# Second FFN's gate and up projections as seven half-size block products per pair of tiles, with the block sums on VectorE

## The chip, the cores and the metric

The kernel runs as one program on one core of a Trainium2 chip. The metric is the device time of one execution in microseconds; lower is better. A core has TensorE (matmuls, called PE in the profile, with its weight loads as PEld), VectorE (DVE), ScalarE (ACT), GpSimd (POOL) and SyncE (SP), which here issues the loads and stores. Each engine works through its own instructions in the order in which they stand, and semaphores make one wait for another.

## What is computed

Two layers of a diffusion backbone over 512 latent tokens, with 256 context tokens beside them in the first layer. Model width is 1024, the hidden width of the FFN 2816. Cut to the part that is changed, the second layer ends with

```python
h_lat = h_lat + g1 * o_lat
a = modulate(rms_norm(h_lat, norm_ffn_g[i]), sh2, sc2)
h_lat = h_lat + g2 * ((silu(a @ ffn_w_gate[i]) * (a @ ffn_w_up[i])) @ ffn_w_down[i])
```

where `a` is 512 x 1024, the gate and up weights are 1024 x 2816 each, and the down weight is 2816 x 1024. Everything is float32.

## The kernel before, in words

A float32 product is made of three matmuls of type fp32r: each operand is split into a high part (a cast) and a low part (the operand minus the cast), and high x high, high x low and low x high are summed in PSUM. Activations lie transposed: channels on the 128 partitions, tokens along the free dimension.

`Weights` streams the weights. A tile of 128 x 1024 float32 is loaded by SP (L134) into one of three raw buffers, cast on ScalarE (L136), and its low part is made on VectorE, or on GpSimd while `W.eng` says so (L137). Four split buffers hold the results, and splits run about two tiles ahead of their use.

The last stage ("stage C", from L1066) begins when the attention of layer two has ended. First comes the output projection `wo_mm` (tiles `pw`, L1102 to L1104), output tiles 0 to 3 with 512 columns, then 4 to 7 in two token halves HA and HB of 256 columns. `updater` adds each into `h` (L555). `Norm.sq` squares on ScalarE (L171) and sums on VectorE (L172, tile `accC`), `Norm.ms` and `Norm.rb` make the root and spread it with small matmuls, and `Norm.apply` makes for each of 8 channel tiles `u` (VectorE, L204), the high part `ahC` (ScalarE, L206) and the low part `alC` (VectorE, L207). During this part `WC.eng` is GpSimd.

Then the FFN. The hidden width is 22 tiles of 128 (j = 0 to 21). For each tile there is a gate unit and an up unit: 8 channel tiles x 3 matmuls of 128 x 128 weights against 512 token columns (`unit_mm`, L118 to L120, PSUM tile `pu`). `first_units` makes the first three units in halves, so that they can start before HB is normed. `elementwise` makes silu (L332), the product (L334), and the split of the result into `hc` (L337, L338). `Down.run` multiplies finished hidden tiles in groups (2, then 4 at a time) by the down weights (PSUM tile `pd`, 512 columns), one group behind the projections. `last_one` does the last four tiles (`pk`, `pd`).

The orders of TensorE and SP are those in which the code is written (`manual_schedule`); those of VectorE, ScalarE and GpSimd are set by a scheduler when the program is built.

Of the kernel before, what the change touches and what calls it, by code (L numbers as in the profile page):

```python
# [11 lines left out]
F32 = mybir.dt.float32  # L12
# [39 lines left out]
def tile_trunk(ctx, tc, hT, cols, rows, rope, mod0, modw, cin, cout, gu, dn0, dn1, dnt, kvin, qin,  # L52
# [4 lines left out]
    hid = ctx.enter_context(tc.tile_pool(name="hid", bufs=1))  # L57
# [102 lines left out]
    class Norm:  # L160
        def __init__(self, layer, sub, hof, acc, tmp, ps):
            self.l, self.s, self.hof, self.acc, self.tmp, self.ps = layer, sub, hof, acc, tmp, ps
            self.x, self.r = {}, {}

        def sq(self, j, st):
            n = width(st)
            if j == 0:
                nc.scalar.activation(out=self.acc[:, st], in_=self.hof(j, st), func=AF.Square)
            else:
                t = self.tmp.tile([P, TL], F32, tag="sq", name="sq")  # L170
                nc.scalar.activation(out=t[:, :n], in_=self.hof(j, st), func=AF.Square)  # L171
                (nc.gpsimd if self.l == 0 and self.s == 0 and st is CTX else nc.vector).tensor_tensor(out=self.acc[:, st], in0=self.acc[:, st], in1=t[:, :n], op=ALU.add)  # L172
# [24 lines left out]
        def apply(self, j, st, ah, al):  # L197
# [5 lines left out]
            u = self.tmp.tile([P, TL], F32, tag="u", name="u")  # L203
# [16 lines left out]
    def first_units(W, n, ah, al, pspool, norm, early):  # L220
        ws = [W.get() for _ in range(n)]
        full = [pspool.tile([P, TL], F32, tag="ps", name="pu") for _ in range(n)]
        res = [{LAT.start: p} for p in full]
        for e, st in enumerate(early):
            for i in range(n):
                if st is CTX:
                    res[i][CTX.start] = pspool.tile([P, TL], F32, tag="ps", name="pu")
                unit_mm(res[i][CTX.start] if st is CTX else full[i][:, st], ws[i], ah, al, st)
                if e == 0 and i == 0:
                    norm.ms(HB)  # L230
                if e == 0 and i == 1:
                    norm.rb(HB)
                    for j in range(ND):
                        norm.apply(j, HB, ah, al)
# [13 lines left out]
    class Down:  # L248
# [24 lines left out]
        def k_outer(self, gi, ws, chunks, st, ms):  # L273
# [3 lines left out]
            for ks in (range(K - 1), (K - 1,)):  # L277
# [310 lines left out]
    o = op.tile([P, ND, TL], F32, name="o")  # L588
    wkv = ctx.enter_context(tc.tile_pool(name="wkv", bufs=1, side="right", reuse_waits="tile"))
# [473 lines left out]
    stB.close()  # L1063

    stC = ExitStack()
    actC = pool(stC, "actC", 1)  # L1066
    ahC = actC.tile([P, ND, TL], F32R, name="ahC")
    alC = actC.tile([P, ND, TL], F32R, name="alC")
    tmpC = pool(stC, "tmpC", 2)
    wrawC = pool(stC, "wrawC", 3)  # L1070
    whlC = pool(stC, "whlC", 4)
    oneC = pool(stC, "oneC", 1)
    psC = pool(stC, "psC", 8, space=PSUM)
    WC = Weights(wrawC, whlC)
    WC.add(wo3[3], 768)
    for m in range(3, ND):
        WC.add(wout[m - 3], 1024)
    ffn_units(WC, 1, dn1)
    table(AF.Silu, live[NI - 1][1][:, 2:3])
    accC = oneC.tile([P, T], F32, name="accC")  # L1080
    oc = []
    for c in range(ND):
        if c < 6:
            oc.append(hid.tile([P, 2, T], F32R, tag="hc", name="hc", bufs=6)[:, :, :TL])
        else:
            oc.append(oneC.tile([P, 2, TL], F32R, name=f"oc{c}"))
# [25 lines left out]
    for i in range(4):  # L1112
        upd(i, LAT, pss[i])
        norm.sq(i, HA)
        norm.sq(i, HB)
    WC.eng = nc.gpsimd
    ws = {m: WC.get() for m in range(4, ND)}
    for st in (HA, HB):
        for i in range(4):
            ps = psC.tile([P, TL], F32, tag="ps", name="pw")  # L1120
# [5 lines left out]
            if st is HB and i == 1:  # L1126
                norm.rb(HA)
                for j in range(ND):
                    norm.apply(j, HA, ahC, alC)
    units = first_units(WC, 3, ahC, alC, psC, norm, (HA,))  # L1130
    WC.eng = nc.vector

    def done(m, st):
        nc.sync.dma_start(out=out[m, :, st], in_=h[:, m, st])

    ffn(WC, 1, ahC, alC, psC, tmpC, (LAT,), updater(1, 5), units, lambda j: None,
        lambda down, gi, chunks: down.last_one(gi, chunks, done))
# [91 lines left out]
```

## Time and profile before

| what | value |
|---|---|
| median of 3 runs | 1661.02 us (1660.96 to 1661.17) |
| span of the profiled execution | 1660.0 us |
| own time of the profiled execution | not listed apart from its span; the runs are 1.0 us above the span |
| PE busy | 1599.6 us, 96% of the span, 9634 matmuls |
| DVE, ACT, POOL busy | 57%, 34%, 14% |
| stage C up to the first unit's HB half | 1233 to 1297 us |
| projections of tile 1 to the start of `last_one` | 1305 to 1634 us |

A busy time is the sum of the recorded durations of an engine's instructions. Matmuls overlap, so their durations say less than the distance from the start of one to the start of the next; this distance is used below for TensorE. The profile's slices of the span give busy shares in tenths and the TensorE clock that was granted.

### The profile page before, as it was taken

The page shows a single profiled execution, that of the slowest core. Times are in us where ns is not written, and L with a number is a line of the kernel's source. Part 1 is how long each engine was busy: PE and PEld are TensorE (multiplying, and loading weights), DVE is VectorE, ACT ScalarE, POOL GpSimd, SP SyncE. Part 2 cuts the span into 40 slices and gives each one's busy share as a digit, 9 for nine tenths or more (in the row PEclk, how much of TensorE's full clock was granted, in tenths as well). Part 3 has the DMA queues.
Part 4 walks back from the last instruction along what each step waited for, and adds up shares of the span by engine and source line. Part 5 has one row for each costly group of instructions (what it writes and reads, how often), then busy time and mean ns, then how long its engine had stood idle before and what let it go on. Part 6 is the DMA issues. An engine that isn't in the chain of part 4 may idle for free.

```text
span 1660.0 us, 23829 instructions
## 1 busy us (share of the span) xinstructions
PE 1599.6 (96%) x9634; PEld 1409.1 (85%) x9634; DVE 946.8 (57%) x1624; ACT 570.2 (34%) x1058; POOL 230.4 (14%) x280
## 2 busy tenths in 40 slices
PE   4999999899999999999999988999989999999999
PEld 3888889898888888888899978988878888888887
DVE  3898654858464443533257488778876443334343
ACT  3422122421212112121235557777763322222221
POOL 4000001200000000000014134566513000000000
PEclk9999999999999999999999999999999999999999
DMA  7565331134234242421103111000022222232231
GB/s 290 201 214 178 115 114 52 52 125 155 102 140 140 102 149 93 143 98 64 58 16 99 46 35 42 1 23 27 1 87 85 77 89 98 93 96 95 90 101 64
DMA packets 47022, 159.81 MB, mean 96 GB/s; under 512 B 5120, under 2 KB 6544, under 8 KB 46784
## 3 DMA queue, kind: packets, MB, share of 16 engines
q1 hardware_dynamic: 46816, 158.06, 27.9%
q8 instruction: 76, 1.25, 0.3%
q0 software_dynamic: 96, 0.23, 0.1%
q14 instruction: 34, 0.28, 0.1%
HBM read 156.17 MB, written 2.10 MB: 95 GB/s over the span
## 4 chain that ended last, share of the span: by engine, by line
PE 87%; DVE 6%; ACT 2%; POOL 2%; issue 1%; DMA 0%; ACTq 0%; DVEq 0%; POOLq 0%
PE pu L119 15%; PE pu L118 15%; PE pu L120 15%; PE pd L118 7%; PE pd L119 7%; PE pd L120 7%; PE pp L1008 2%; PE pp L1021 1%; PE s L985 1%; PE s L984 1%; PE s L983 1%; DVE al L207 1%; PE pp L1020 1%; PE pu L217 1%; PE pw L1104 1%
## 5 line engine op out<-in xcount | busy, mean ns | idle before, releaser
L136 ACT CAST wh<-wr 128x1024 fp32r<-128x1024 f32 (+2 forms) x180 | 186.7, 1038 | 587.9 <-PE pu L120 228.6
L118 PE MATMUL pu<-ah,wh 128*128 128x256 f32 (+1 forms) x1040 | 347.8, 334 | 0.0
L119 PE MATMUL pu<-al,wh 128*128 128x256 f32 (+1 forms) x1040 | 347.6, 334 | 0.0
L120 PE MATMUL pu<-ah,wh 128*128 128x256 f32 (+1 forms) x1040 | 347.5, 334 | 0.0
L137 DVE TENSOR_TENSOR wh<-wr,wh 128x1024 fp32r<-128x1024 f32 (+1 forms) x152 | 187.2, 1233 | 217.2 <-ACT wh L136 216.9
L118 PE MATMUL pd<-hc,wh 128*128 128x256 f32 (+1 forms) x676 | 228.4, 338 | 0.0
L119 PE MATMUL pd<-hc,wh 128*128 128x256 f32 (+1 forms) x676 | 227.9, 337 | 0.0
L120 PE MATMUL pd<-hc,wh 128*128 128x256 f32 (+1 forms) x676 | 227.3, 336 | 0.0
L119 PEld LDWEIGHTS pu<-al,wh 128*128 128x128 f32 x1040 | 196.4, 189 | 22.4
L118 PEld LDWEIGHTS pu<-ah,wh 128*128 128x128 f32 x1040 | 196.2, 189 | 22.4
L120 PEld LDWEIGHTS pu<-ah,wh 128*128 128x128 f32 x1040 | 196.4, 189 | 22.2
L508 DVE CUSTOM_DVE_ANT_0 junk<-modr,cb 128x1024 f32<-128x1024 f32 x128 | 156.2, 1221 | 58.3 <-DMA modr<-in_modw 57.3
L137 POOL TENSOR_TENSOR wh<-wr,wh 128x1024 fp32r<-128x1024 f32 (+1 forms) x28 | 63.8, 2289 | 843.5 <-ACT wh L136 843.4
L119 PE MATMUL pu<-alC,wh 128*128 128x512 f32 (+1 forms) x352 | 138.3, 393 | 2.7 <-DVE alC L207 2.7
L118 PEld LDWEIGHTS pd<-hc,wh 128*128 128x128 f32 x676 | 128.3, 190 | 14.4
L119 PEld LDWEIGHTS pd<-hc,wh 128*128 128x128 f32 x676 | 128.4, 190 | 13.9
L120 PEld LDWEIGHTS pd<-hc,wh 128*128 128x128 f32 x676 | 128.2, 190 | 14.1
L555 DVE SCALAR_TENSOR_TENSOR h<-pd,M,h 128x512 f32<-128x512 f32 (+1 forms) x125 | 84.2, 675 | 96.4 <-PE pd L120 96.4
L118 PE MATMUL pu<-ahC,wh 128*128 128x512 f32 (+1 forms) x352 | 138.1, 392 | 0.4 <-ACT ahC L206 0.4
L120 PE MATMUL pu<-ahC,wh 128*128 128x512 f32 (+1 forms) x352 | 137.8, 391 | 0.0
L334 DVE TENSOR_TENSOR sg<-sg,pu 128x256 f32<-128x256 f32 (+1 forms) x66 | 39.5, 598 | 146.1 <-PE pu L120 128.2
L332 ACT ACTIVATE sg<-pu 128x256 f32<-128x256 f32 (+1 forms) x66 | 34.8, 528 | 207.1 <-PE pu L120 207.1
(233 smaller groups left out, 2780.5 us busy)
## 6 DMA issues: line engine op xcount, KB each, us to landing
wr<-in_gu SPq DMA_DIRECT2D x88, 512.0 KB, 3.5
modr<-in_modw SPq DMA_DIRECT2D x80, 512.0 KB, 4.3
wr<-in_dn SPq DMA_DIRECT2D x40, 512.0 KB, 3.5
wr<-in_cin SPq DMA_DIRECT2D x24, 512.0 KB, 4.6
mw<-in_mod SPq DMA_DIRECT2D x16, 512.0 KB, 9.4
wrb<-in_qup SPq DMA_DIRECT2D x12, 384.0 KB, 3.1
wr<-in_cout SPq DMA_DIRECT2D x8, 512.0 KB, 4.0
wr<-in_qin SPq DMA_DIRECT2D x6, 512.0 KB, 3.6
```

The costliest lines, as they stand in the source:

```text
L118: nc.tensor.matmul(ps, wh, xh, start=i == 0, stop=False)
L119: nc.tensor.matmul(ps, wh, xl, start=False, stop=False)
L120: nc.tensor.matmul(ps, wl, xh, start=False, stop=i == n - 1)
L136: nc.scalar.copy(out=w[:, 0, :n], in_=r[:, :n])
L137: (eng or self.eng).tensor_tensor(out=w[:, 1, :n], in0=r[:, :n], in1=w[:, 0, :n].bitcast(F32), op=ALU.subtract)
L207: nc.vector.scalar_tensor_tensor(out=al[:, j, st], in0=u[:, :n], scalar=sh, in1=ah[:, j, st].bitcast(F32), op0=ALU.add, op1=ALU.subtract)
L217: nc.tensor.matmul(ps, wh, al[:, k, st], start=False, stop=False)
L332: nc.scalar.activation(out=sg[:, st], in_=g[st.start][:, :width(st)], func=AF.Silu)
L334: nc.vector.tensor_tensor(out=sg[:, st], in0=sg[:, st], in1=u[st.start][:, :width(st)], op=ALU.mult)
L508: nc.vector.tensor_tensor_reduce(out=junk, in0=r, in1=cb[:, st], scale=1.0, scalar=0.0, op0=ALU.mult, op1=ALU.add, accum_out=M[:, l, st, s ...
L555: nc.vector.scalar_tensor_tensor(out=hof(m, st), in0=ps, scalar=M[:, layer, i, s, m:m + 1], in1=hof(m, st), op0=ALU.mult, op1=ALU.add)
L1008: nc.tensor.transpose(ps[:, e], pr[:, tok(3 * b + e)], ident)
```

## The change

Tiles 0 and 1 are computed as before. Tiles 2 to 21 are computed in ten pairs. For a pair, gate and up are each a product of a 256 x 1024 weight block by a 1024 x 512 activation block. Each is cut in two by two: the weights into A11, A12 (tile p, first and second 512 channels) and A21, A22 (tile q), the activations into B11, B12, B21, B22 (channel half, token half). Seven products of a 128 x 512 block by a 512 x 256 block replace eight, in a form of Strassen's method (Winograd's variant).

- The activation sums t1 to t4 are made once (`combo`), on VectorE with casts on ScalarE. They need the whole `a` in float32, so `Norm.apply` writes a copy `af` with a second activation per tile.
- The weight sums are made per pair on VectorE, in place in the raw tiles (`Stream.pair`, `add`), before the split of the block.
- The result blocks are put together in PSUM by accumulating several products into one bank (A), with copies out to SBUF between them (ScalarE), and sums on VectorE (tile `c`).
- `Stream` replaces `Weights` in stage C: blocks of 512 columns, 7 raw buffers, 9 split buffers, splits up to 8 blocks ahead. The splits under `WC.eng` on GpSimd become 14 of half size in place of 7.
- `last_one` leaves the last two hidden tiles of its group to the end in its first half, not the last one (`late=2`).
- Pools are opened in another order, so that `hid` and `wkv` give their memory back before stage C.

The core of the diff:

```diff
+        def half(self):
+            while len(self.ready) <= self.ahead and self.todo:
+                self._split()
+            return self.ready.pop(0)
...
+            for step in range(7):
+                for p, q in ids:
+                    a11, a12, a21, a22 = (p, 0), (p, 512), (q, 0), (q, 512)
+                    if step == 0:
+                        self.block(*a11, 512)
+                    elif step == 1:
+                        self.block(*a12, 512)
+                    elif step == 2:
+                        self.block(*a21, 512, chain(add(a11, a11, a21), add(a21, a21, a22)))
+                    elif step == 3:
+                        self.block(*a21, 512, add(a21, a11, a22))
+                    elif step == 4:
+                        self.block(*a11, 512)
+                    elif step == 5:
+                        self.block(*a22, 512)
+                    else:
+                        self.block(*a12, 512, chain(add(a12, a12, a21), done(p, 2), done(q, 1)))
...
             nc.scalar.activation(out=ah[:, j, st], in_=u[:, :n], func=AF.Identity, bias=sh)
             nc.vector.scalar_tensor_tensor(out=al[:, j, st], in0=u[:, :n], scalar=sh,
                                            in1=ah[:, j, st].bitcast(F32), op0=ALU.add, op1=ALU.subtract)
+            if full is not None:
+                nc.scalar.activation(out=full[:, j, st], in_=u[:, :n], func=AF.Identity, bias=sh)
...
-    wrawC = pool(stC, "wrawC", 3)
-    whlC = pool(stC, "whlC", 4)
+    wrawC = pool(stC, "wrawC", 7)
+    whlC = pool(stC, "whlC", 9)
...
+    combo(B[0, 0], t1[:, 0], t1[:, 1], lambda: nc.vector.tensor_tensor(
+        out=B[0, 0], in0=B[0, 0], in1=B[0, 1], op=ALU.subtract))
...
+    def product(ps, x, first=False):
+        w = WC.half()
+        xh, xl = X[x]
+        for k in range(4):
+            wh, wl = w[:, 0, k * P:(k + 1) * P], w[:, 1, k * P:(k + 1) * P]
+            nc.tensor.matmul(ps, wh, xh[:, k], start=first and k == 0, stop=False, skip_group_check=not first)
+            nc.tensor.matmul(ps, wh, xl[:, k], start=False, stop=False, skip_group_check=not first)
+            nc.tensor.matmul(ps, wl, xh[:, k], start=False, stop=k == 3, skip_group_check=not first)
...
+        for g in range(2):
+            product(A[g], "b11", True)
+            nc.scalar.copy(out=cs_[g][:, 0], in_=A[g])
+        Bk = bank()
+        for g in range(2):
+            product(Bk[g], "b21", True)
+            nc.vector.tensor_tensor(out=cs_[g][:, 0], in0=cs_[g][:, 0], in1=Bk[g], op=ALU.add)
+        Dk = bank()
+        for g in range(2):
+            product(Dk[g], "t1", True)
+        for g in range(2):
+            product(A[g], "t2")
+            nc.scalar.copy(out=cs_[g][:, 1], in_=A[g])
+        for g in range(2):
+            product(A[g], "t3")
+            nc.scalar.copy(out=cs_[g][:, 2], in_=A[g])
+            nc.vector.tensor_tensor(out=cs_[g][:, 2], in0=cs_[g][:, 2], in1=Dk[g], op=ALU.add)
+        for g in range(2):
+            product(A[g], "t4")
...
+        for g in range(2):
+            product(Dk[g], "b22")
+            nc.vector.tensor_tensor(out=cs_[g][:, 1], in0=cs_[g][:, 1], in1=Dk[g], op=ALU.add)
...
+    for j in range(2, NJ, 2):
+        fast_pair(j)
+        if j == GROUPS[gi][1]:
+            down.run(gi, [chunks.pop(k) for k in range(*GROUPS[gi])])
+            gi += 1
```

Order of the instructions, first place: VectorE in the projections of two tiles far from a down group, before. `wh<-wr,wh` are splits of weights, `sg` and `hc` the elementwise work.

```order
L334 TENSOR_TENSOR sg<-sg,pu 128x512
L137 TENSOR_TENSOR wh<-wr,wh 128x1024
L338 TENSOR_TENSOR hc<-sg,hc 128x512
L137 TENSOR_TENSOR wh<-wr,wh 128x1024
L334 TENSOR_TENSOR sg<-sg,pu 128x512
```

The same engine in a pair that is followed by another pair, from the splits for the next pair on (`wr<-wr` are the weight sums, `c` the result sums):

```order
L191 TENSOR_TENSOR wh<-wr,wh 128x512 x3
L211 TENSOR_TENSOR wr<-wr 128x512 x2
L191 TENSOR_TENSOR wh<-wr,wh 128x512 x2
L211 TENSOR_TENSOR wr<-wr 128x512
L1341 TENSOR_TENSOR c<-c,pf 128x256
L191 TENSOR_TENSOR wh<-wr,wh 128x512
L211 TENSOR_TENSOR wr<-wr 128x512
L1341 TENSOR_TENSOR c<-c,pf 128x256
L191 TENSOR_TENSOR wh<-wr,wh 128x512
L1348 SCALAR_TENSOR_TENSOR sg<-c,sg 128x256
```

Where one split stood between two elementwise instructions, there now stand splits, weight sums and result sums in turn; the result sums stand behind splits for blocks that are used eight products later.

Second place: VectorE at the start of the first pair, where before the last `alC` of the norm were followed by `sg<-sg,pu`. L1293 to L1301 are the activation sums and their low parts, with `af` the copy.

```order
L311 SCALAR_TENSOR_TENSOR alC<-u,M,ahC 128x256 x4
L1297 TENSOR_TENSOR af<-af 128x4x256
L1293 TENSOR_TENSOR t_12554<-af,t_12554 128x1024
L1299 SCALAR_TENSOR_TENSOR af<-af 128x4x256
L211 TENSOR_TENSOR wr<-wr 128x512
L1301 SCALAR_TENSOR_TENSOR af<-af 128x4x256
L1282 TENSOR_TENSOR sg<-sg,pu 128x512
L211 TENSOR_TENSOR wr<-wr 128x512
L1293 TENSOR_TENSOR t_11758<-af,t_11758 128x1024
L211 TENSOR_TENSOR wr<-wr 128x512
L1293 TENSOR_TENSOR t_12555<-af,t_12555 128x1024
L1293 TENSOR_TENSOR alC<-af,ahC 128x4x256
```

Behind these rows come `hc`, a sum, `sg<-sg,pu` and the first two weight splits that VectorE makes for the first pair; they now stand behind all of the activation sums.

Third place: GpSimd's last instructions. Before, five of its seven splits in stage C stood behind the first root (`rs`):

```order
L137 TENSOR_TENSOR wh<-wr,wh 128x1024 x4
L101 TENSOR_TENSOR rs<-rs,nhalf 128x2
L137 TENSOR_TENSOR wh<-wr,wh 128x1024
```

and now

```order
L191 TENSOR_TENSOR wh<-wr,wh 128x512 x3
L102 TENSOR_TENSOR rs<-rs,nhalf 128x2
L191 TENSOR_TENSOR wh<-wr,wh 128x512 x7
L102 TENSOR_TENSOR rs<-rs,nhalf 128x2
L191 TENSOR_TENSOR wh<-wr,wh 128x512 x4
```

The last four splits of half size stand behind the second root, where one split of full size stood.

## Rows read from the trace of the kernel before

**Rows 1.** The page: busy time of PE, then the 40 slices of DVE and of the clock
```profile
PE 1599.6 (96%) x9634; PEld 1409.1 (85%) x9634; DVE 946.8 (57%) x1624; ACT 570.2 (34%) x1058; POOL 230.4 (14%) x280
...
DVE  3898654858464443533257488778876443334343
...
PEclk9999999999999999999999999999999999999999
```

**Rows 2.** Windows: stretch, its us, busy us of PE, PEld, DVE, ACT, POOL; clock, DMA
```profile
1278.69:1296.60 17.91, 14.83 (x82) 13.74 (x81) 10.31 (x20) 4.88 (x11) 4.10 (x3) 0.71 0.21 68
1296.60:1305.15 8.55, 8.55 (x75) 8.55 (x73) 4.31 (x11) 2.93 (x7) 0.00 (x0) 1.00 0.01 2
1305.15:1634.19 329.04, 329.04 (x1418) 266.81 (x1417) 130.47 (x142) 85.06 (x104) 2.42 (x1) 1.00 0.29 95
```

**Rows 3.** Timeline of PE: start us, us, line, out<-in, [idle before <-releaser]
```profile
1255.00 0.28 PE L1102 MATMUL pw<-hc,wh 128*128 128x256 f32 x1
...
1266.43 0.28 PE L1102 MATMUL pw<-hc,wh 128*128 128x256 f32 x1
...
1305.15 0.39 PE L118 MATMUL pu<-ahC,wh 128*128 128x512 f32 x1
...
1634.19 0.39 PE L282 MATMUL pk<-hc,wh 128*128 128x512 f32 x1
```

**Rows 4.** Groups by shape, DVE, 1310 to 1650 us: xcount | busy us, mean ns | idle before
```profile
L555 DVE SCALAR_TENSOR_TENSOR h<-pd,M,h 128x512 f32<-128x512 f32 x41 | 30.6, 750 | 41.6 <-PE pd L120 41.6
L338 DVE TENSOR_TENSOR hc<-sg,hc 128x512 fp32r<-128x512 f32 x22 | 15.0, 684 | 0.0
```

**Rows 5.** Groups by shape, DVE, whole span: 256 columns
```profile
L334 DVE TENSOR_TENSOR sg<-sg,pu 128x256 f32<-128x256 f32 x22 | 9.3, 421 | 11.4 <-PE pu L120 11.4
L555 DVE SCALAR_TENSOR_TENSOR h<-pd,M,h 128x256 f32<-128x256 f32 x34 | 16.2, 478 | 5.6 <-PE pd L120 5.6
```

**Rows 6.** Groups by shape, ACT: the first two 1310 to 1650 us, then whole span
```profile
L136 ACT CAST wh<-wr 128x1024 fp32r<-128x1024 f32 x59 | 61.8, 1047 | 161.7 <-PE pd L120 62.7 <-PE pu L120 59.7 <-issue 36.6
L337 ACT CAST hc<-sg 128x512 fp32r<-128x512 f32 x21 | 12.9, 615 | 0.0
...
L804 ACT COPY kcat<-pp 128x256 f32<-128x256 f32 x24 | 9.1, 381 | 0.0
L206 ACT ACTIVATE ahC<-u,M 128x256 fp32r<-128x256 f32 x16 | 7.5, 503 | 15.6 <-DVE u L204 15.6
```

**Rows 7.** Timelines of DVE and POOL around the norm of stage C
```profile
1265.54 0.43 DVE L172 TENSOR_TENSOR accC<-accC,sq 128x256 f32<-128x256 f32 x1 [0.55 <-ACT sq L171]
...
1270.88 2.58 DVE L172 TENSOR_TENSOR accC<-accC,sq 128x256 f32<-128x256 f32 x1 [0.84 <-ACT sq L171]
...
1280.62 2.19 DVE L172 TENSOR_TENSOR accC<-accC,sq 128x256 f32<-128x256 f32 x1
...
1270.80 2.39 POOL L137 TENSOR_TENSOR wh<-wr,wh 128x1024 fp32r<-128x1024 f32 x1
...
1280.07 2.46 POOL L137 TENSOR_TENSOR wh<-wr,wh 128x1024 fp32r<-128x1024 f32 x1 [0.44 <-ACT wh L136]
```

**Rows 8.** Timeline of PE in the first unit's HA half and after it
```profile
1278.69 0.28 PE L118 MATMUL pu<-ahC,wh 128*128 128x256 f32 x1
...
1284.05 0.58 PE L119 MATMUL pu<-alC,wh 128*128 128x256 f32 x1 [2.37 <-DVE alC L207]
...
1288.49 0.41 PE L120 MATMUL pu<-ahC,wh 128*128 128x256 f32 x1
1288.71 0.41 PE L118 MATMUL pu<-ahC,wh 128*128 128x256 f32 x1
```

**Rows 9.** DMA issues: xcount, KB each, median us from issue to landing
```profile
wr<-in_gu SPq DMA_DIRECT2D x88, 512.0 KB, 3.5
```

**Rows 10.** Timeline of DVE: a wait for ScalarE, and two instructions in a row
```profile
1295.02 0.89 DVE L207 SCALAR_TENSOR_TENSOR alC<-u,M,ahC 128x256 fp32r<-128x256 f32 x2 [0.19 <-ACT ahC L206]
...
1310.36 0.68 DVE L338 TENSOR_TENSOR hc<-sg,hc 128x512 fp32r<-128x512 f32 x1
1310.96 0.68 DVE L334 TENSOR_TENSOR sg<-sg,pu 128x512 f32<-128x512 f32 x1
```

More of the change, by code (lines that the diff above doesn't have):

```diff
@@ L195, in rb, with apply @@
                 self.r[st.start] = rb[:, :n]
-        def apply(self, j, st, ah, al):
+        def apply(self, j, st, ah, al, full=None):
             n = width(st)
@@ L233, in first_units @@
                     for j in range(ND):
-                        norm.apply(j, HB, ah, al)
+                        norm.apply(j, HB, ah, al, whole)
         for k in range(ND):
@@ L276, in k_outer @@
             part = [self.ps.tile([P, TL], F32, tag="ps", name="pk")[:, :n] for _ in ms]
-            for ks in (range(K - 1), (K - 1,)):
+            for ks in (range(K - late), range(K - late, K)):
                 for i, m in enumerate(ms):
@@ L1115, in tile_trunk @@
         norm.sq(i, HB)
+    af = op.tile([P, ND, TL], F32, tag="o", name="af")
     WC.eng = nc.gpsimd
-    ws = {m: WC.get() for m in range(4, ND)}
+    ws = {}
     for st in (HA, HB):
         for i in range(4):
+            if st is HA:
+                ws[4 + i] = WC.get()
             ps = psC.tile([P, TL], F32, tag="ps", name="pw")
@@ L1128, in tile_trunk @@
                 for j in range(ND):
-                    norm.apply(j, HA, ahC, alC)
-    units = first_units(WC, 3, ahC, alC, psC, norm, (HA,))
+                    norm.apply(j, HA, ahC, alC, af)
+    units = first_units(WC, 3, ahC, alC, psC, norm, (HA,), af)
     WC.eng = nc.vector
@@ L1134, in done, with split_pair @@
         nc.sync.dma_start(out=out[m, :, st], in_=h[:, m, st])
-    ffn(WC, 1, ahC, alC, psC, tmpC, (LAT,), updater(1, 5), units, lambda j: None,
-        lambda down, gi, chunks: down.last_one(gi, chunks, done))
+    down = Down(WC, GROUPS, psC, (LAT,), updater(1, 5))
+    chunks = {}
+    def split_pair(j, sg):
+        hc = hc_pair()
+        for e in range(2):
+            nc.scalar.copy(out=hc[:, e, 0], in_=sg[:, e])
+            nc.vector.tensor_tensor(out=hc[:, e, 1], in0=sg[:, e], in1=hc[:, e, 0].bitcast(F32), op=ALU.subtract)
+            chunks[j + e] = hc[:, e]
@@ new lines, in tile_trunk @@
+    units.append(unit(WC, ahC, alC, psC, (LAT,)))
+    sg = tmpC.tile([P, 2, TL], F32, tag="sg", name="sg")
+    for e in range(2):
+        nc.scalar.activation(out=sg[:, e], in_=units[2 * e][0], func=AF.Silu)
+        nc.vector.tensor_tensor(out=sg[:, e], in0=sg[:, e], in1=units[2 * e + 1][0], op=ALU.mult)
+    split_pair(0, sg)
+    K1, K2 = slice(0, 4), slice(4, 8)
+    B = {(k, n): af[:, (K1, K2)[k], (HA, HB)[n]] for k in range(2) for n in range(2)}
+    t1 = oneC.tile([P, 2, 4, TL // 2], F32R, tag="t1", name="t1")
@@ new lines, in tile_trunk, with combo @@
+    t4 = oneC.tile([P, 2, 4, TL // 2], F32R, name="t4")
+    def combo(src, hi, lo_, *f):
+        f[0]()
+        nc.scalar.copy(out=hi, in_=src)
+        nc.vector.tensor_tensor(out=lo_, in0=src, in1=hi.bitcast(F32), op=ALU.subtract)
+    combo(B[0, 0], t1[:, 0], t1[:, 1], lambda: nc.vector.tensor_tensor(
+        out=B[0, 0], in0=B[0, 0], in1=B[0, 1], op=ALU.subtract))
+    combo(B[0, 1], ahC[:, K1, HB], alC[:, K1, HB], lambda: nc.vector.tensor_tensor(
+        out=B[0, 1], in0=B[1, 1], in1=B[0, 1], op=ALU.subtract))
@@ new lines, in fast_pair, with bank @@
+    def fast_pair(j):
+        def bank():
+            return [psC.tile([P, TL], F32, tag="ps", name="pf")[:, :NH2] for _ in range(2)]
+        cs_ = [tmpC.tile([P, T], F32, tag="c", name="c", bufs=5).rearrange("p (a n) -> p a n", a=3)
+               for _ in range(2)]
+        sg = tmpC.tile([P, 2, TL], F32, tag="sg", name="sg")
+        A = bank()
+        for g in range(2):
[17 more added lines that the diff above has]
+            product(A[g], "t4")
+            if g == 0:
+                nc.scalar.activation(out=sg[:, 1, HB], in_=cs_[0][:, 2], func=AF.Silu, scale=-1.0)
+                nc.scalar.activation(out=sg[:, 1, HA], in_=A[0], func=AF.Silu, scale=-1.0)
+            else:
+                nc.vector.scalar_tensor_tensor(out=sg[:, 1, HB], in0=cs_[1][:, 2], scalar=-1.0, in1=sg[:, 1, HB],
+                                               op0=ALU.mult, op1=ALU.mult)
+                nc.vector.scalar_tensor_tensor(out=sg[:, 1, HA], in0=A[1], scalar=-1.0, in1=sg[:, 1, HA],
+                                               op0=ALU.mult, op1=ALU.mult)
+        for g in range(2):
+            product(Dk[g], "b22")
+            nc.vector.tensor_tensor(out=cs_[g][:, 1], in0=cs_[g][:, 1], in1=Dk[g], op=ALU.add)
+            both = cs_[g][:, 0:2].rearrange("p a n -> p (a n)")
+            if g == 0:
+                nc.scalar.activation(out=sg[:, 0], in_=both, func=AF.Silu)
+            else:
+                nc.vector.tensor_tensor(out=sg[:, 0], in0=sg[:, 0], in1=both, op=ALU.mult)
+        split_pair(j, sg)
@@ L1138, in tile_trunk @@
+    gi = 0
+    for j in range(2, NJ, 2):
[3 more added lines that the diff above has]
+            gi += 1
+    down.last_one(gi, [chunks.pop(k) for k in range(*GROUPS[gi])], done)
     stC.close()
```

133 lines of the change are left out of this document (113 added, 20 removed).

## The prediction

> **What bounds the kernel now.** I read the page first [rows 1]: PE is busy 96% of the span, DVE 57%, and in the last nine slices (the part that is changed) DVE stands at three or four tenths with the clock in the top tenth. Then the windows [rows 2]: from 1305.15 to 1634.19 PE has no idle time in 329.04 us, at a clock of 1.00; DVE works 130.47 us of it (40%), ACT 85.06 (26%), POOL 2.42, DMA 29%. So the end is set there by the number and size of the matmuls alone, and everything else has room. The stretch before it is different: 1278.69 to 1296.60, the first units while the norm is being made, takes 17.91 us at a clock of 0.71. Last come the timelines: [rows 3] for what a matmul costs, [rows 7, 8, 10] for what holds the norm up.
>
> **Price of a matmul.** Durations overlap, so I take distances between starts [rows 3]. With 512 columns: (1634.19 - 1305.15) / 1416 = 0.2324 us. With 256 columns: (1266.43 - 1255.00) / 96 = 0.1191; the HB halves of three units confirm it, 72 matmuls in 8.55 us = 0.1188 [rows 2]. Half the columns thus cost half, but for 2 x 0.119 - 0.2324 = 0.006 us, although every matmul has its own weight load in both cases.
>
> **The main term.** A pair of tiles had 2 tiles x 2 projections x 24 = 96 matmuls of 512 columns: 96 x 0.2324 = 22.31 us. Now 7 products x 2 projections x 4 channel tiles x 3 = 168 of 256 columns: 168 x 0.1190 = 19.99. It saves 2.32 us a pair, **23.2 us** for ten, while the kernel makes 720 matmuls more. All of it lies on the path, since PE never waits there.
>
> **What DVE has to do for it.** Per pair, by durations: 14 half-size splits, 8 weight sums and 2 splits of `hc`, all of 512 elements with two SBUF operands, 24 x 0.684 = 16.4 us [rows 4]; the product of silu and up, 0.7; six result sums of 256 columns with one operand in PSUM, 6 x 0.421 = 2.5, and two three-operand ones, 2 x 0.478 = 1.0 [rows 5]. That is 20.6. The share of the down projection per pair (4 updates at 0.750, and 4 half-size splits) adds 5.7: 26.3. PE needs 19.99 for the pair and 48 x 0.2324 = 11.16 for the down part: 31.1. DVE rises from 40% to about 26.3 / 31.1 = 85% by durations, or 75% by start distances (two such instructions in a row start 0.60 apart, though each lasts 0.68 [rows 10]). It stays under PE. Two pairs without a down group between them ask 41.2 + 5.5 for the next weights = 46.7 us by durations, 41 by distances, of 40.0 us of PE; the lead of eight blocks (8 x 0.684 = 5.5 us of splits) covers that. ACT has per pair 14 casts at 0.615, the copies at 0.381 [rows 6], silu and casts of `hc`: about 16 us of 31. It costs nothing.
>
> **Waits inside a pair.** Products t2, t3 and t4 of one gate add into bank A, with ScalarE's copy between them. The copy (0.38) has one product of the other projection to be done in, 12 x 0.119 = 1.43 us, less a hand-over of 0.2 on each side [rows 10]; slack about 0.7. But ScalarE and VectorE work in order: in the order above a result sum stands behind splits and weight sums (up to 1.4 us), and where silu waits for such a sum, ScalarE's copy behind it waits too. The next user is two or more products away, so mostly it is hidden. I take **+1.5 us** over ten pairs; ends 0 (hidden all over) and +10 (one split of 0.684 plus a hand-over, about 1 us, in every pair).
>
> **The norm.** At full clock, 1278.69 to 1296.60 would hold 72 x 0.119 = 8.6 us and some ten small matmuls, about 9.2; 8.7 us are lost. Rows show how: a sum of squares takes 0.43 us alone, and 2.58 and 2.19 while GpSimd's splits (2.39, 2.46) run [rows 7]; PE then waits 2.37 us for `alC`, and afterwards goes at half clock, starts 0.22 apart [rows 8]. After the change, GpSimd's splits are of half size (about 1.2 us, estimated from 2.4), so a sum waits less at a time. Against it, ScalarE gets a second activation per tile and half (16, about 0.5 each by `ahC` [rows 6]). Laid out by hand with these durations, HB starts about 1291 to 1292 instead of 1296.60; as the order of GpSimd against VectorE can come out otherwise, I take **-3 us**, ends -5.3 (that layout) and +2 (16 activations behind `ahC`, a quarter of their 8 us not hidden).
>
> **Start of the first pair.** The order's second place shows eight instructions of 1024 elements on VectorE for the activation sums (about 1.2 us each, twice the 0.60 of [rows 10]), ahead of the first weight splits that VectorE makes. From the start of HB, VectorE has 4.31 us of its old work [rows 2], 9.6 of sums, three weight sums and two splits (5 x 0.68 = 3.4): 17.3. The product t1 comes 8.55 + 24 x 0.2324 + 4 x 1.43 = 19.8 us after the same point. So it is just in time if nothing holds VectorE. But GpSimd's last four half-size splits (the order's third place) follow the second root and fall beside these sums: 4 x 1.2 = 4.8 us in which a VectorE instruction with two SBUF operands can be held, as in [rows 7]. Then the t1 products come 4.8 - 2.5 = 2.3 us late, and what follows some 0.7 more: **+3 us**. Ends: 0, and +7.4, if PE also falls to half clock after that wait, as it did after 2.37 us [rows 8]: 10 us at 0.22 instead of 0.119 lose 4.4. The Trainium skill ("SBUF — State Buffer", section "Who interferes with whom") says that a VectorE instruction with two SBUF inputs and a GpSimd one that reads SBUF lock each other out for a whole instruction; [rows 7] agree, 2.58 against 2.39. Nearly every instruction that the change adds to VectorE is of that kind, but by that rule the harm ends where GpSimd's splits end.
>
> **Edits at no cost.** The weights are the same bytes in as many loads; a load lands in 3.5 us [rows 9], and eight blocks ahead is about 11 us; DMA is at 29% [rows 2]. If that lead were gone, 3.5 us a load would show. The end: with two tiles kept back, 24 x 0.2324 = 5.6 us of matmuls cover sum 0.42, product 0.69, cast 0.62 and split 0.68 = 2.4 us [rows 4 to 6]. `last_one` and the output are otherwise as before.
>
> **Sum.** Against the profiled execution: 1660.0 - 23.2 - 3 + 3 + 1.5 = 1638.3 us. The runs' median stands 1.0 above that span, so **1639 us**.
>
> **Rivals.**
> A. In-order waits give more back: the sums inside a pair stall PE by 1 us each pair (+10 in place of 1.5), or the first pair starts late and at half clock (+7.4 in place of 3), or both: 1639 + 4.4 to + 13, so 1643 to 1652. For it: the rows of the order, where `c` stands behind splits. Against it: results are wanted about two products later. Chance 0.2.
> B. VectorE becomes the bound, and it is slower than before. Mechanism: each of its instructions waits for a partner on ScalarE (cast to split, copy to sum), with no queue of ready work. Such a hand-over was 0.19 us [rows 10]. Per pair 41 instructions x 0.19 + 26.3 = 34.1 us, more than the 31.1 + 2.3 = 33.5 that a pair and its down part took before; ten pairs at +0.6 plus the 1.5: 1661 + 7.5, near 1668. It decides from (33.5 - 26.3) / 41 = 0.175 us an instruction. For it: 85% busy leaves little. Against: weight sums need no ScalarE, casts run eight blocks ahead, and rows without a wait start 0.60 apart. Chance 0.06.
> C. Half-size matmuls don't take half the time in this order, with weights that change at each: for a fixed part of 0.0138 us more (2.32 / 168) the gain is gone, and at 0.02 a pair loses 1.0: 1661 + 10 = 1671. Against: the 96 matmuls of [rows 3] had a weight load each. The Trainium skill ("TensorE: Matmul & The Clock Gate", section "Back-to-back issue gap") gives about 81 ns at 128 columns and 131 at 512 for such streams, so halving would not halve; by that rule a pair would cost far more than before. The trace disagrees: 119 and 232 ns. Chance 0.02.
> D. The norm gains what the hand layout gives and the first pair starts in time: 1639 - 2.3 - 3 - 1.5, about 1632. Chance 0.1.
>
> **Numbers.** The forecast (1635 to 1643) keeps 0.62. The range takes D and most of A: 1631 to 1651. A measurement can tell about 0.2%, 3.3 us, from no change. Faster by more: forecast, D and A up to 1652, 0.62 + 0.1 + 0.18 = 0.9; within: 0.04 (both ends of A's costs with a VectorE near its bound); slower: B and C with what they don't hold, 0.06.
>
> **What would show it.** Matmuls to tile `pf` 0.119 apart at a clock near 1.0; in the last stage PE idle under 5 us, DVE at 75 to 85%; HB of the first units starting before 1294; the wait at the first pair's t1 about 2 us. It is wrong if PE waits for `c`, `wh` or bank A in every pair, if the clock falls below 0.95 there, or if the stretch up to HB has not become shorter.

## The result, and the profile after

The changed kernel takes 1639.73 us (median of 4 runs, 1637.36 to 1642.53) against 1661.1 in the same session: ratio 0.9875, 95% interval 0.9861 to 0.9889. Predicted were 1639. The profiled execution took 1639.27 us with a span of 1637.4, so its time lies 1.9 above its span where 1.0 was assumed.

First the page of the changed kernel: busy time of the engines, then the slices of VectorE.

```profile
PE 1574.7 (96%) x10354; PEld 1426.3 (87%) x10354; DVE 1064.4 (65%) x1907; ACT 647.1 (40%) x1280; POOL 235.3 (14%) x287
...
DVE  3898654857554353533338388777885798778774
```

Against [rows 1] PE makes 720 more matmuls and is busy 25 us less; VectorE's last nine slices went from 3 or 4 tenths to between 7 and 9, but for the very last one. The windows tell where this lies (the first is the first units, HA to tile 1, the second two pairs with no down part between them, the third tile 1 to `last_one`):

```profile
1281.89:1303.14 21.25, 18.89 (x154) 18.25 (x153) 17.03 (x31) 13.74 (x32) 7.76 (x5) 1.00 0.15 48
...
1404.92:1444.80 39.88, 39.88 (x338) 39.87 (x336) 31.64 (x57) 24.60 (x49) 0.00 (x0) 1.00 0.42 140
1303.14:1611.50 308.36, 306.74 (x2139) 285.77 (x2137) 248.36 (x412) 153.65 (x296) 6.10 (x4) 1.00 0.28 95
```

Beside [rows 2]: the first units took 26.46 us (17.91 + 8.55) and take 21.25; tile 1 to `last_one` took 329.04 and takes 308.36. Two pairs take 39.88 us, PE without a gap, VectorE busy 31.64 of them. The timeline of PE gives the borders (1294.60 is where HB of the first units begins) and every wait after the output projection that is over 0.25 us:

```profile
1235.96 0.39 PE L1231 MATMUL pw<-hc,whb 128*128 128x512 f32 x1
...
1281.89 0.28 PE L119 MATMUL pu<-ahC,wh 128*128 128x256 f32 x1
...
1285.13 0.39 PE L120 MATMUL pu<-alC,wh 128*128 128x256 f32 x1 [0.83 <-DVE alC L311]
...
1286.94 0.39 PE L120 MATMUL pu<-alC,wh 128*128 128x256 f32 x1 [1.10 <-DVE alC L311]
...
1287.88 0.61 PE L282 MATMUL ms<-ones,accC 128*128 128x1 f32 x4 [0.44 <-DVE accC L276]
...
1294.60 0.28 PE L322 MATMUL pu<-ahC,wh 128*128 128x256 f32 x1
...
1303.14 0.39 PE L119 MATMUL pu<-ahC,wh 128*128 128x512 f32 x1
...
1308.72 0.28 PE L1313 MATMUL pf<-ahC,wh 128*128 128x256 f32 x1
...
1319.93 0.38 PE L1315 MATMUL pf<-t,wh 128*128 128x256 f32 x1 [0.55 <-DVE wh L191]
...
1322.41 0.39 PE L1313 MATMUL pf<-ahC,wh 128*128 128x256 f32 x1 [1.03 <-ACT c L1337]
...
1611.50 0.39 PE L388 MATMUL pk<-hc,wh 128*128 128x512 f32 x1
```

From these, the ledger of the two profiled executions against the sum of the prediction:

| term | predicted | measured | from |
|---|---|---|---|
| ten pairs, 96 x 512 columns to 168 x 256 | -23.2 | -23.7 | 22.31 to 39.88 / 2 = 19.94 a pair |
| first pair | +3 | +2.4 | 1308.72 to 1331.06 (first `pd`) = 22.34, less 19.94 |
| waits in the other nine | +1.5 | +0.6, none of it a wait | 308.36 - 329.04 + 23.7 - 2.4 |
| norm and first units | -3 | -5.2 | 26.46 to 21.25 |
| all ahead of the first unit | 0 | +3.2 | 1278.69 to 1281.89 |
| `last_one` to the end | 0 | +0.1 | 25.81 to 25.90 |
| sum | -21.7 | -22.6 | span 1660.0 to 1637.4 |

The +0.6 is no wait: from the first `pd` (1331.06) to `last_one` PE is busy 280.44 us of 280.44. Most of it lies in the second and third pair, which took 40.33 us (start to start) where the two behind them took 39.88; in the repeat below they took 39.86.

So the total was right to a microsecond, but two terms were off by more than that, one of them put at nothing in the prediction, and they cancelled in part. The experiments go after these, and after the room that VectorE and PE's main term really have.

### The profile page after: what moved, and what is told of

Same layout as the page of the kernel before. It is cut to its first block, busy times and chain, and to the rows that moved or that the text cites. A ratio compares the mean times of both kernels' runs of the same rounds, so it can differ in the third digit from the quotient of the medians.

```text
span 1637.4 us, 25955 instructions
## 1 busy us (share of the span) xinstructions
PE 1574.7 (96%) x10354; PEld 1426.3 (87%) x10354; DVE 1064.4 (65%) x1907; ACT 647.1 (40%) x1280; POOL 235.3 (14%) x287
## 4 chain that ended last, share of the span: by engine, by line
PE 85%; DVE 7%; ACT 2%; POOL 2%; issue 2%; DMA 0%; ACTq 0%; POOLq 0%; DVEq 0%
PE pu L119 11%; PE pu L121 11%; PE pu L120 11%; PE pd L119 7%; PE pd L120 7%; PE pd L121 7%; PE pf L1313 4%; PE pf L1315 4%; PE pf L1314 4%; PE pp L1115 2%; PE pp L1128 1%; PE s L1091 1%; PE s L1092 1%; PE pw L1231 1%; PE pw L1232 1%
## 5 line engine op out<-in xcount | busy, mean ns | idle before, releaser
L137 ACT CAST wh<-wr 128x1024 fp32r<-128x1024 f32 (+1 forms) x108 | 111.7, 1034 | 414.5 <-PE pu L121 170.2
L138 DVE TENSOR_TENSOR wh<-wr,wh 128x1024 fp32r<-128x1024 f32 x87 | 107.3, 1233 | 109.9 <-ACT wh L137 109.6
L190 ACT CAST wh<-wr 128x512 fp32r<-128x512 f32 x204 | 124.5, 619 | 122.4 <-PE pd L121 59.2
L191 DVE TENSOR_TENSOR wh<-wr,wh 128x512 fp32r<-128x512 f32 x190 | 128.2, 687 | 63.5 <-ACT wh L190 62.4
L138 POOL TENSOR_TENSOR wh<-wr,wh 128x1024 fp32r<-128x1024 f32 (+1 forms) x21 | 46.8, 2239 | 798.0 <-ACT wh L137 798.0
L1313 PE MATMUL pf<-ahC,wh 128*128 128x256 f32 x320 | 90.1, 282 | 1.0 <-ACT c L1337 1.0
L1315 PE MATMUL pf<-ahC,wh 128*128 128x256 f32 x320 | 90.3, 282 | 0.0
L1314 PE MATMUL pf<-alC,wh 128*128 128x256 f32 x320 | 90.2, 282 | 0.0
```

The source lines that it names most:

```text
L137: nc.scalar.copy(out=w[:, 0, :n], in_=r[:, :n])
L138: (eng or self.eng).tensor_tensor(out=w[:, 1, :n], in0=r[:, :n], in1=w[:, 0, :n].bitcast(F32), op=ALU.subtract)
L190: nc.scalar.copy(out=w[:, 0, :n], in_=r)
L191: self.eng.tensor_tensor(out=w[:, 1, :n], in0=r, in1=w[:, 0, :n].bitcast(F32), op=ALU.subtract)
L1313: nc.tensor.matmul(ps, wh, xh[:, k], start=first and k == 0, stop=False, skip_group_check=not first)
L1314: nc.tensor.matmul(ps, wh, xl[:, k], start=False, stop=False, skip_group_check=not first)
```

## Experiments

### The changed kernel again

> The changed kernel once more, unchanged, for its spread and to see which of its stretches repeat. Theory: the ledger of the first trace is fixed by the order of the instructions, so it repeats within 0.3 us: first units from HA to tile 1 in 21.25 us, first pair 22.34, each later pair 19.94, and the 1.99 us wait for pt near 1187 in the attention stage. Rival: the late start of the last stage (3.2 us later than in the kernel before) is chance, as the clock fell in two places; then HA starts near 1278.7 this time.

1638.13 us (1636.11 to 1638.23), ratio 0.9861 (0.9847 to 0.9876). The first pair again took 22.33 us and the wait of 1.99 us for `pt` came again, but the first units took 23.82 us instead of 21.25, with the same waits (0.82 and 1.10), the output projection began at 1232.89, 3.1 us earlier, and HA at 1278.81, which is where the rival put it. The windows of the two traces in the first units show why; first this run:

```profile
1283.00:1291.00 8.00, 6.99 (x32) 6.70 (x33) 2.51 (x6) 0.04 (x1) 0.83 (x2) 0.57 0.15 58
...
1278.81:1302.63 23.82, 21.76 (x154) 21.03 (x153) 17.03 (x31) 13.74 (x32) 7.77 (x5) 0.86 0.13 43
```

and the same stretch in the first trace:

```profile
1286.00:1294.00 8.00, 6.62 (x53) 6.42 (x54) 4.64 (x12) 1.65 (x5) 0.91 (x2) 1.00 0.16 60
```

32 matmuls in 8 us at a granted clock of 0.57 against 53 at 1.00. The waits are fixed by the order; whether the clock falls to its lower level (1.2 GHz) after them is not, and that is worth 2.6 us here. "Repeats within 0.3 us" held for the pairs and the wait for `pt`, but neither for the first units nor for the start of the last stage. The rival was right on that start, but not that chance is all of it: the 1.99 us came again.

### The kernel before again

> The kernel before once more, for its profile. Theory (PE's clock falls or not after a wait by chance, the order of waits is fixed): the same waits of 0.28, 0.43 and 2.37 us in the first units, the stretch from HA to tile 1 between 23 and 27 us by the clock, no wait of 1.99 us for pt, output projection from 1230 to 1233.5. Rival (the figures of the first trace repeat to 0.3 us): 26.5 us and 1233.0.

Its one run took 1662.73 us. Waits 0.28, 0.43 and 2.37, no 1.99, projection from 1232.52, first units 26.53 us:

```profile
1278.15:1304.68 26.53, 23.46 (x155) 22.38 (x154) 14.61 (x30) 7.80 (x17) 4.08 (x3) 0.81 0.14 44
```

The clock is again 0.81 over the stretch. The run does not decide between theory and rival, as 26.5 us fits both and 1232.52 misses the rival's 1233.0 by little. With the first trace, both of this kernel have the slower clock there; of ten traces of the changed kernel and its variants five have it (22.7 to 24.1 us) and five don't (20.6 to 21.3). Ordered by the longest wait of PE in the stretch, over all traces here: the four with a wait of 1.50 to 2.37 us all have it, of the eight with 1.09 or 1.10 four have it, and the one with 0.78 does not.

### Half-size splits on GpSimd, alone

```diff
-            (eng or self.eng).tensor_tensor(out=w[:, 1, :n], ...)
+            for lo in range(0, n, 512 if self.halves and e is nc.gpsimd else n):
+                hi = min(n, lo + (512 if self.halves and e is nc.gpsimd else n))
+                e.tensor_tensor(out=w[:, 1, lo:hi], ...)
```

> The kernel before with one edit: GpSimd's splits of the last stage are made as two instructions of half size. Theory (half-size splits hold VectorE's sums up for a shorter time, and this is what shortened the norm): the stretch from HA to tile 1 goes from 26.46 us to 21 to 23, and the time from 1661 to 1656 to 1658. Rival (the stretch became shorter because the change has another order and other splits there): 26 to 27 us, and 1661 within 1.

1659.91 us, ratio 0.9992 (0.9983 to 1.0002): not to be told from no change, so by time the theory's 1656 to 1658 missed. In the trace the stretch took 24.32 us, between the theory's 23 and the rival's 26 (its window, then its longest wait):

```profile
1276.24:1300.56 24.32, 22.07 (x154) 20.98 (x153) 13.75 (x30) 7.80 (x16) 4.80 (x4) 0.86 0.17 56
...
1280.73 0.58 PE L119 MATMUL pu<-alC,wh 128*128 128x256 f32 x1 [1.50 <-DVE alC L211]
```

The waits fell from 3.08 us (0.28 + 0.43 + 2.37) to 2.24 (0.31 + 0.43 + 1.50). That is about what the whole change has (0.83 + 1.10 + 0.44 = 2.37), so the shorter GpSimd instructions are worth 0.7 to 0.8 us of waits; the rest of the 5.2 us was the clock (0.81 before, 0.86 here, 1.00 in the first trace of the change). The count above suggests, and does not show, that shorter waits make its fall rarer, so that this part is not all luck.

### All of the change but the seven products

```diff
-            WC.pair([(gu[1, j, g], gu[1, j + 1, g]) for g in range(2)])
+            for e in range(2):
+                for g in range(2):
+                    WC.std(gu[1, j + e, g], 1024)
...
-        fast_pair(j)
+        plain_pair(j)
```

> The changed kernel without the seven products: blocks, buffers, norm with the copy, and late=2 stay, but tiles 2 to 21 are projected as in the kernel before, 96 matmuls of 512 columns a pair, with no activation, weight or result sums. Theory (seven products are worth 2.37 us a pair less the waits of 2.9): 1637.4 + 23.7 - 2.9 = 1658 us of span, 1659 to 1660 of time. Rival (the first units' gain of 5.2 us comes from the change as a whole and not from its blocks of half size): the stretch from HA to tile 1 is again 26 us, span 1663. Rival 2 (the late start of the last stage belongs to the sums): HA at 1278.7, span 1655.

1657.81 us, ratio 0.9982 (0.9973 to 0.9991), span 1657.8.

```profile
1282.33:1302.95 20.62, 18.70 (x154) 18.23 (x153) 11.45 (x25) 12.79 (x31) 7.77 (x7) 1.00 0.18 64
1302.95:1632.00 329.05, 329.05 (x1419) 266.82 (x1417) 139.40 (x201) 97.75 (x163) 1.48 (x2) 1.00 0.27 87
```

Tile 1 to `last_one` is back at 329.05 us, as in [rows 2] (329.04) to the hundredth. So the seven products are worth 20.7 us in the trace (19.7 by the medians, 1657.81 to 1638.13) and nothing else in the change touches that stretch. The first units keep their gain (20.62) and the late start stays (1236.41): neither belongs to the sums.

### 36 of 168 matmuls left out

```diff
-        for k in range(4):
+        for k in ((3,) if x in ("t4", "b22") else range(4)):
```

> The changed kernel, of whose products with t4 and with b22 only one channel tile of four is computed: 36 of 168 matmuls a pair are left out, all other work stays. Theory (PE alone sets the steady pairs, VectorE has 48.9 us of 62.2 in two pairs and their down part): ten times 36 x 0.1187 = 4.27, so 40 to 43 us less, near 1598. Rival (hand-overs between VectorE, ScalarE and PE are close to the limit, and VectorE is next at 48.9 of 53.7): less than 30 us less, with PE waiting for wh or c in every pair.

1601.28 us, ratio 0.9634 (0.9619 to 0.9648): 36.9 less than the repeat of the changed kernel, a little under the theory's 40. From the first `pd` to `last_one` 245.87 us against 280.44, so 34.57 / 9 = 3.84 us a pair where 4.27 were taken out. The missing 0.43 us is in the main one gap in each of the nine pairs, ahead of the second t4 product (0.39 us from start to start where 0.12 is usual); in four of them a second gap follows (0.17 to 0.41), ahead of the second b22 product. PE, then ScalarE:

```profile
1352.79 0.29 PE L1315 MATMUL pf<-t,wh 128*128 128x256 f32 x1
1353.18 0.39 PE L1313 MATMUL pf<-t,wh 128*128 128x256 f32 x1
...
1352.75 0.37 ACT L1340 COPY c<-pf 128x256 f32<-128x256 f32 x1 [0.55 <-PE pf L1315]
```

The second t4 product starts when the copy of bank A ends (1353.12). The product of the other projection that hides this copy had been cut from 1.43 us to 0.36: the copies between products cost nothing only because a whole product covers them. The rival's wait for `c` in every pair is there, but small. VectorE did not become the bound, though its mean load in these 245.87 us was 215.72, 88%.

### More work for VectorE

Each of these repeats weight splits (same result): eight of the fourteen, or all.

```diff
+            for _ in range(2 if again else 1):
                 self.eng.tensor_tensor(out=w[:, 1, :n], in0=r, ...)
...
+                self.again = step in (1, 3, 4, 5)
```

> The changed kernel, in which VectorE makes eight of the fourteen weight splits of each pair twice: 8 x 0.60 = 4.8 us more of VectorE a pair. Theory (room of 6.6 us a pair on average, 4.1 in a pair without a down part, a lead of eight blocks): 0 to 4 us more in all. Rival (VectorE is as good as the bound): 4.8 a pair, up to 48 us more.

> All fourteen splits of each pair made twice: 8.4 us more of VectorE a pair. Theory (VectorE becomes the bound when 48.9 + 16.8 = 65.7 us exceed 62.2 for two pairs and their down part): 3.5 us for each of the four such groups and some at the start, 14 to 22 us more. Rival (hidden anyway): under 4. Rival (bound already): 80.

1645.78 us (ratio 0.9906, 0.9891 to 0.9920) and 1667.81 us (ratio 1.0039, 1.0025 to 1.0054), 7.7 and 29.7 more than the repeat. Where it lies, for eight (first pair, then the rest up to `last_one`):

```profile
1309.92:1337.66 27.74, 23.42 (x169) 22.68 (x168) 27.19 (x42) 15.03 (x31) 4.45 (x3) 0.88 0.29 102
1337.66:1620.30 282.64, 280.60 (x1947) 260.78 (x1945) 259.50 (x446) 134.72 (x262) 0.00 (x0) 1.00 0.26 93
```

and for fourteen (the rest, then the first pair):

```profile
1340.02:1641.07 301.05, 287.93 (x1946) 265.81 (x1945) 289.60 (x503) 134.96 (x264) 0.00 (x0) 0.98 0.25 91
1310.05:1340.02 29.97, 24.12 (x170) 22.29 (x168) 29.86 (x44) 14.79 (x29) 8.02 (x4) 0.89 0.18 62
```

Nine pairs with 4.8 us more VectorE each lost 2.2 us in all (282.64 against 280.44): that room is there, as reckoned. With 8.4 more they lost 20.6, VectorE busy 289.60 of 301.05: that is the bound, and these nine pairs alone lie in the range expected for everything (14 to 22). Both lose more in the first pair, 27.74 and 29.97 us against 22.34 (5.4 and 7.6), since VectorE has no room there (busy 22.34 of 22.34 us in the changed kernel) and the clock fell (0.88 and 0.89); for that reason 0 to 4 for eight and 14 to 22 for fourteen were too low in all. With all fourteen made twice the kernel is slower than the one before: the gain stands on some 6 us of room a pair.

### An edit for a shorter lead that did not shorten it

```diff
-    WC = Stream(wrawC, whlC, 7, 7)
+    WC = Stream(wrawC, whlC, 7, 2)
```

> The changed kernel with splits three blocks ahead of their use in place of eight; buffers as they are. Theory (the lead covers the stretches in which VectorE works through sums, two pairs without a down part among them): waits for wh of 0.3 to 2 us a pair, 3 to 20 us more. Rival (what counts is only VectorE's mean load of 79%): within 2 us.

1637.56 us, ratio 0.9858 (0.9842 to 0.9875), the same as the repeat. From the first `pd` on 280.44 us, as without the edit, with PE never idle. All waits of PE from the first pair to `last_one` lie in the first pair (22.88 us for 22.34):

```profile
PE pf L1313 <- ACT wh L190: 1.0, 1, 1.0
PE pf L1313 <- ACT c L1337: 0.8, 1, 0.8
PE pf L1315 <- DVE wh L191: 0.2, 1, 0.2
```

This looks like the rival, but it does not decide. VectorE in two pairs and the down part after them, with the shorter lead,

```profile
1403.14:1443.02 39.88, 39.88 (x338) 39.87 (x336) 31.64 (x57) 24.66 (x49) 0.00 (x0) 1.00 0.41 141
1443.02:1465.33 22.31, 22.31 (x99) 18.09 (x98) 17.24 (x27) 5.61 (x9) 0.00 (x0) 1.00 0.10 33
```

does in each the same number of instructions (57 and 27 rows) in the same time as without the edit (31.64 and 17.24 us). The orders of VectorE and ScalarE are set by the scheduler, and from the first pair's middle on they are the same in both kernels: there the number that was changed does not set the lead. What does is argued and not shown: the nine split buffers are the limit that is left, and no run has fewer of them. What the lead is worth stays open.

### GpSimd off the activation sums

```diff
+            if self.eng is nc.gpsimd:
+                self.npool += 1
+                if self.npool > 10:
+                    self.eng = nc.vector
```

> The changed kernel, but GpSimd makes 10 of its 14 splits and VectorE the last four, which lay beside the activation sums. Theory (GpSimd's reads hold VectorE there): the four at 0.60 cost VectorE 2.4 us, the three instructions at 1.77, 2.31 and 1.19 that took 0.68, 1.2 and 0.68 give back 2.7 and those before 1304 as much again; the waits of the first pair fall from 2.4 us to 1 or less, time 1 to 2 us less. Rival (VectorE's queue, not GpSimd, makes the first pair late): the waits stay at 2.4 or grow to 4.

1638.19 us, ratio 0.9864 (0.9847 to 0.9880): the time did not move, the stretch did. The first pair took 21.09 us (22.34), and only 0.48 us of wait for the copy is left. In the changed kernel, VectorE, ScalarE and GpSimd had:

```profile
1304.08 1.77 DVE L211 TENSOR_TENSOR wr<-wr 128x512 f32<-128x512 f32 x1 [1.18 <-POOL wh L191]
1305.77 2.31 DVE L1301 SCALAR_TENSOR_TENSOR af<-af 128x1024 f32<-128x1024 f32 x1
...
1317.83 4.26 ACT L190 CAST wh<-wr 128x512 fp32r<-128x512 f32 x8 [1.57 <-DVE wr L211]
1322.00 0.36 ACT L1337 COPY c<-pf 128x256 f32<-128x256 f32 x1
...
1299.57 9.68 POOL L191 TENSOR_TENSOR wh<-wr,wh 128x512 fp32r<-128x512 f32 x4 [10.11 <-ACT wh L190]
```

and here VectorE has

```profile
1307.16 1.22 DVE L1306 SCALAR_TENSOR_TENSOR af<-af 128x1024 f32<-128x1024 f32 x1
```

The same sum (L1301 in one kernel, L1306 in the other) takes 1.22 us alone and 2.31 beside GpSimd, and GpSimd's four half-size splits take 2.42 on average (9.68 / 4) beside VectorE, where [rows 7] have about that for one of full size. The Trainium skill's page "SBUF — State Buffer" (section "Who interferes with whom") says that a VectorE instruction with two SBUF inputs contends with a GpSimd one that reads SBUF. The trace agrees: 2.31 us against 1.22. The other wait has another cause: in ScalarE's order the copy of bank A stood behind eight casts that had waited for one weight sum. That part is left here: 0.48 us of the 1.03.

### The splits of the attention's output

In the table, 3.2 us were lost ahead of the first unit. The changed kernel's trace has, near 1181 us in the attention stage, five casts and five splits of its output almost in a row (ScalarE, VectorE), and PE behind them, waiting for `pt`, an operand of the attention that VectorE makes after those splits:

```profile
1181.06 1.68 ACT L1216 CAST hc<-o 128x512 fp32r<-128x512 f32 x3
...
1182.99 1.16 ACT L1216 CAST hc<-o 128x512 fp32r<-128x512 f32 x2
...
1181.73 1.90 DVE L1217 TENSOR_TENSOR hc<-o,hc 128x512 fp32r<-128x512 f32 x3
...
1184.88 1.28 DVE L1217 TENSOR_TENSOR hc<-o,hc 128x512 fp32r<-128x512 f32 x2
1186.08 0.55 DVE L1117 TENSOR_TENSOR pt<-pp,pt 128x384 fp32r<-128x384 f32 x1
...
1186.69 0.41 PE L1009 MATMUL pp<-ident,kcat 128*64 128x128 f32 x2 [1.99 <-DVE pt L1117]
```

In the kernel before, four of them were made 34 us earlier, two by two and one by one, ScalarE:

```profile
1146.65 1.15 ACT L1087 CAST hc<-o 128x512 fp32r<-128x512 f32 x2
...
1149.32 0.61 ACT L1087 CAST hc<-o 128x512 fp32r<-128x512 f32 x1
...
1150.62 0.65 ACT L1087 CAST hc<-o 128x512 fp32r<-128x512 f32 x1
```

There they went into buffers of `hid`; now they go into a new pool opened after `hid` is closed. One line was moved:

```diff
+    oneC = pool(stC, "oneC", 1)
     hid = pool(stC, "hidC", 1)
...
-    oneC = pool(stC, "oneC", 1)
```

> The changed kernel with one line moved: the pool with the sums' tiles is opened ahead of the pool for hc, so that the splits of the attention's output stand at the end of the attention stage in VectorE's and ScalarE's order (six in a row) and not five in a row near 1181 us. Theory (the five in a row make PE wait 1.99 us for pt and its clock fall, which is why the last stage starts 3 us later than in the kernel before): that wait is gone, the output projection starts 2 to 3 us earlier than in the other runs of the changed kernel (their mean is 1235.0), and the time is 1 to 3 us less, unless the six at the end cost as much: a cast and a split ahead of the first matmul, about 1.3 us. Rival (the late start is the clock's chance): no wait of 1.99 us near 1187, but the same start within 1 us and the same time.

1636.89 us (1634.1 to 1638.68), ratio 0.9862 (0.9845 to 0.9878): by time not to be told from the repeat. In the trace the 1.99 us are gone, and the projection starts at 1228.06, against a mean of 1235.0 over the eight traces with the five in a row (1232.89 to 1236.77). It pays for that with 1.35 us more than usual over its first part (23.45 us for 22.10), 0.76 of them in a wait for a weight's cast; the other trace with the line moved (next section) starts at 1230.96 and does not pay it (22.11 us).

The clock also varies ahead of this stage, so the start alone does not tell the order from chance. TensorE's order there is the same in all kernels, though, and the same stretch of it can be compared. It holds the same 457 matmuls in every trace, from the 71st to the 105th of 117 groups of `pp<-ident,pr`; in the kernel before, the changed one and this one:

```profile
1136.40 0.38 PE L1008 MATMUL pp<-ident,pr 128*128 128x128 f32 x2
...
1203.30 0.38 PE L1008 MATMUL pp<-ident,pr 128*128 128x128 f32 x2
...
1134.92 0.38 PE L1115 MATMUL pp<-ident,pr 128*128 128x128 f32 x2
...
1204.28 0.38 PE L1115 MATMUL pp<-ident,pr 128*128 128x128 f32 x2
...
1133.51 0.38 PE L1115 MATMUL pp<-ident,pr 128*128 128x128 f32 x2
...
1197.95 0.38 PE L1115 MATMUL pp<-ident,pr 128*128 128x128 f32 x2
```

That is 66.90, 69.36 and 64.44 us. All traces fall into three groups that do not overlap: 66.7 to 66.9 with the order of the kernel before (three traces), 68.2 to 69.6 with the five in a row (eight), 64.4 and 64.6 with the line moved (two). So of the 3.2 us some 2.5 come with the order, which includes what the clock lost after the wait, and the moved line gives back more than that. The rest, 0.7 us in these two traces, lies outside the stretch and changes from run to run: the repeat of the changed kernel lost 2.3 us in it (69.22) and still reached HA where the kernel before did.

### Both together

> The line moved as above, and GpSimd with 10 in place of 14 splits. Theory: both gains add up, 1.25 us in the first pair and 1 to 3 us ahead of the last stage: 1634 to 1637. Rival: 1638 as the changed kernel.

1634.23 us (1632.39 to 1635.80), ratio 0.9842 (0.9827 to 0.9856). This beats the kernel before, and lies under the first measurement of the changed kernel (0.9861 to 0.9889); it overlaps the interval of the repeat (0.9847 to 0.9876) at its edge, so that the gain of the two together, expected and found at 1634 to 1637, is likely and not shown. Projection from 1230.96, first units at full clock, first pair 21.09:

```profile
1276.89:1298.15 21.26, 18.91 (x155) 18.27 (x153) 17.29 (x32) 13.74 (x32) 4.20 (x4) 1.00 0.14 48
...
1303.73:1324.82 21.09, 20.59 (x170) 20.18 (x168) 21.03 (x37) 13.00 (x27) 0.00 (x0) 1.00 0.39 148
```

## Why the prediction was right, and where not

- **Price of a matmul, main term**: right. 19.94 / 168 = 0.1187 us in the new order, as read from [rows 3] and [rows 2]. Rival C is out, and the undone version gives the stretch back to 0.01 us.
- **VectorE's load**: right. 48.9 us of 62.2 for two pairs and their down part (31.64, and 17.24 in the down part's 22.3), 79%, between the two values given. Rival B needed an added 0.175 us for each instruction, so that VectorE would be the bound; with eight more splits a pair it still was not, and nine pairs lost 2.2 us.
- **Two pairs without a down part**: right in the result (no wait), rough in the working. VectorE was reckoned to have 41 to 46.7 us of work there; it had 31.64, and 17.24 in the down part of 22.3 us, whose own eight updates are some 6 (8 x 0.750 of [rows 4]). So some 11 us of the pairs' work lay in the down part, more than the 5.5 of a lead of eight blocks. That it needs this lead was not shown.
- **Waits inside a pair**: none for +1.5 in the nine pairs behind the first; the +0.6 of the table are not waits. The mechanism of rival A (in-order queues) came once, in the first pair: 1.03 us for a copy behind eight casts. The copies of bank A are hidden by one product, as argued, and the run with cut products showed what it costs without (0.43 us a pair).
- **Start of the first pair**: +2.4 for +3, about half of it by the mechanism named (1.25 of it goes with GpSimd's last four splits). The rest was not named there: a copy behind casts in ScalarE's order. The waits fell on t2 and t3, not on t1.
- **The norm**: the sign was right, the term "-3" mis-sized: -5.2 in the profiled execution. The step held the shorter GpSimd splits responsible; alone they take 0.8 us off the waits. The rest is the clock, which stayed up in that execution and not in the repeat (23.82 us, a gain of 2.6). The sign "HB before 1294" failed by 0.6 us (1294.60), since the stage began later; from HA to HB it took 12.71 us for 17.91.
- **Ahead of the last stage**: "Edits at no cost" left out the pools' order altogether, and that cost some 2.5 us, in a stage that the change does not compute in. The text of the change named it; the order of ScalarE in the attention stage, had it been read there, shows the five casts in a row.

The last two errors had opposite signs, and the runs' median stood 2.3 us above the profiled span where 1.0 was assumed, which hides that the span came out 0.9 us lower than forecast. The forecast of 1639 is therefore better than its parts: that it was met to a microsecond is luck, the main term is not.

## What to carry to other kernels

Where PE is never idle and everything else has room, fewer columns times matmuls is the time saved, and block sums on another engine are free until that engine's load comes near PE's: reckon it over a whole period, with the part in which PE does something else. Then look for cost at the seams: the first period, before any queue is full, and the stages ahead, where a new pool's memory decides when earlier results may be split. On in-order queues, ask of every copy that PE waits for what stands in front of it.

## What the runs showed that was not expected

After the same waits of 0.82 and 1.10 us in the first units, PE's clock fell to half in some executions and not in others (0.57 and 1.00 in the same 8 us), which moves the time by some 2.6 us. The changed kernel's runs spread over 5 us, and a gain of 1.25 us that the trace shows plainly (first pair, 22.34 to 21.09) could not be seen in its time. Nor does the clock's fall look like pure chance: it fell in all four traces with a wait of 1.50 to 2.37 us in the first units, and in half of the eight with 1.09 or 1.10.
